# Width of the projection matmuls for the second half of the tokens: 512 columns instead of two groups of 256

## The chip, the cores and the metric

The kernel runs on one core of a Trainium2 chip. The metric is the time of one execution on the device in microseconds (us), given as the median of the runs. The engines are named as in the profile: PE (TensorE, with PEld for its weight loads), DVE (VectorE), ACT (ScalarE), POOL (GpSimd) and SP, whose queue issues nearly all DMAs.

## What is computed

One block of a network on x of 2048 tokens by 1024 features, in float32, cut here to what matters:

```python
h = rms_norm(x, norm_g) * (1.0 + scale) + shift
p = h @ w_in                                  # 2048 x 5960: all projections in one product
(pr, pk, pv, pwd, pad_, z_a, q, ckv, z_b, qi, ki, wi, g_a, g_b) = split(p)   # the first 1664 columns after a token shift
y_a = rwkv7_branch(pr, pk, pv, pwd, pad_, ...)            # a recurrence over the tokens
y_b = dsa_branch(q, ckv, qi, ki, wi, ...)                 # index scores, the best 256 keys, attention over them
br_a = (y_a * silu(z_a)) @ w_pa
br_b = (y_b * silu(z_b)) @ w_pb
merged = sigmoid(g_a) * br_a + sigmoid(g_b) * br_b
out = rms_norm(x + gate * (merged @ w_o), final_g)
```

## The kernel before

The tokens are cut into four blocks of 512 (`TB`), the features of x into eight groups of 128 (`KD`). Operands are split into a high and a low part (`whi`, `wlo` for weights, `hh`, `hl` for the transposed and normed h), and a product is made of three matmuls: high by high, high by low, low by high.

A *unit* of the projection GEMM is one group of 128 output columns for one block of 512 tokens. It fills one PSUM bank `g` (two buffers) with 3 x 8 products. `self.cut` says in how many groups of columns the bank is filled, one group after the other, each with its own accumulation:

```python
        w = TB // self.cut
        for c in range(self.cut):
            s = slice(c * w, c * w + w)
            n = 0
            for k in range(KD):
                for a, b in ((hi, hh), (hi, hl), (lo, hh)):
                    T.matmul(p[:, s], a[:, k], b[:, k, s], start=n == 0, stop=n == 3 * KD - 1)
                    n += 1
```

After a unit, `evacuate` takes the whole bank away: kind "s" (the columns of the recurrence) with ACT L333 and DVE L334, kind "q" with ACT L264 and DVE L265 (`split_out`), the latent columns with `latent` (L356 to L367), and kinds "z" and "g" (gates) with the ACT copy L347 alone. All write to DRAM.

`gemm_half` is called for the first two blocks of tokens with all kinds, and then for the last two with "rkv" (13 groups of columns), "q" (5) and "z", "g" (24). That makes 84 units for the first half, 84 for the second, and 20 more for the index projections (`gemm_index`), which run first.

Around the second half's GEMM stands the recurrence. For each block of tokens, `rwkv_pass` (from L607) prepares factors, `rwkv_inv` inverts triangular blocks on DVE (L733 and the reduction behind it), and `rwkv_chain` (from L742) goes through eight chunks of 64 tokens, each of which needs the state that the one before left: PE L781 and L784, ACT copy L787, PE L790, DVE copy L791, PE L794, DVE L799, PE L801. `heads` (L868, L878) prepares keys and values. After the GEMM, `branch_a` (L1092) makes the first branch's output projection in eight blocks of 256 tokens, and then `attention` and `finish` follow.

The order of instructions on each engine isn't written out by hand. The scheduler of the language sets it when the kernel is built: it goes through the program by an estimated timeline, and of the instructions that are ready on an engine takes that with the lowest number in `self.band(...)`: the passes and inversions of the blocks 0 and 1 and the first chain from 50000, later passes, inversions and chains from 55000, the projections "rkv" 60000, `heads` 65000, the projections "q", "z", "g" 70000, `branch_a` 75000, attention 80000. Weight loads and evacuations go before all else (`urgent`). On the chip each engine then runs its instructions in the order that was set.

Of the kernel before, what the change touches and what calls it, by code (L numbers as in the profile page):

```python
# [25 lines left out]
FR = mybir.dt.float32r  # L26
# [5 lines left out]
PSUM = bass.MemoryType.PSUM  # L32
DRAM = bass.MemoryType.DRAM
# [11 lines left out]
LOWEST = -1.0e38  # L45
# first columns of the projections
C_R, C_K, C_V, C_WA = 0, 512, 1024, 1536
# [4 lines left out]
class Block:  # L52
# [19 lines left out]
    def move(self, dst, src, q=None):  # L72
        """a DMA of float32r words as they are"""
        f = [a.bitcast(FT) if a.dtype == FR else a for a in (dst, src)]
        return (q or self.nc.sync).dma_start(f[0], f[1])
# [3 lines left out]

    # ---------------------------------------------------------------- constants  # L80
    def consts(self):
# [5 lines left out]
        DMA.dma_start(self.ident, x["k_ident"])  # L87
        # scratch in DRAM
        self.QIS = d.tile([8, 128, S], FR, name="qis")
# [21 lines left out]

    # ---------------------------------------------------------------- start: modulation, norm, h^T
    def start(self):
# [32 lines left out]
        for tb in range(NTB):  # L146
# [23 lines left out]
            if tb >= 2:  # L170
                self.move(self.HHS[tb - 2], hh, q=G)
                self.move(self.HLS[tb - 2], hl, q=G)
        # the last third of the modulation is for the end
        acc = self.ada(w, cT, 2, [])
# [7 lines left out]
        DMA.dma_start(self.GT, ab)  # L182
        # bias by distance; beyond the last bucket's start it is constant and drops out of the softmax
        rb, bk, br = (w.tile([32, n], FT, name="b%d" % i, bufs=1) for i, n in enumerate((8, 384, 384)))
# [11 lines left out]
    def ada(self, w, cT, j, ahead):  # L196
        """a third of the modulation, partial sums by partition"""
        nc = self.nc
        acc = w.tile([128, D], FT, name="acc")
        for k in range(KD):  # L200
            aw = w.tile([128, D], FT, name="x", bufs=7)
            m = nc.sync.dma_start(aw, self.x["ada_w"][k * 128:(k + 1) * 128, j * D:(j + 1) * D])
            if j == 0:
                self.shift_in = m.ins
            if k == 0:
                nc.vector.tensor_scalar(acc, aw, cT[:, 0:1], None, op0=OP.mult)
            else:
                nc.vector.scalar_tensor_tensor(acc, aw, cT[:, k:k + 1], acc, op0=OP.mult, op1=OP.add)
            if ahead:
                ahead.pop(0)()  # L210
        return acc

    # ---------------------------------------------------------------- the projection GEMM
    @contextmanager
    def urgent(self):
        """what frees or feeds the tensor engine goes before all else"""
        p = self.tc.cur_priority
# [37 lines left out]
    def split_out(self, p, scale=None, rows=128):  # L255
        """FR hi and lo of a PSUM tile."""
        nc, w = self.nc, self.wp
# [43 lines left out]
    def gemm_half(self, tbs, kinds):  # L301
# [4 lines left out]
        for kind in kinds:  # L306
# [6 lines left out]
            if kind == "g":  # L313
                jobs += [("g", i, C_GA + i * 128) for i in range(16)]
        # at the turn of the halves, a block of tokens serves two columns at a time
        n = len(jobs)
# [53 lines left out]

    # ---------------------------------------------------------------- index scores and the selection
    def select(self):
        """For each query the mask of its TOPK best keys (ties go to the lower index).

        A threshold is sought by the secant method on the count of scores at or above it, until the count is
        at most eight short of TOPK; the missing ones are then the largest below the threshold. Where the
        search has not ended so, a branch finds the TOPK-th largest value bit by bit.
        """
        nc, tc = self.nc, self.tc
        V, A, T, G, DMA = nc.vector, nc.scalar, nc.tensor, nc.gpsimd, nc.sync  # L380
        MID = TOPK - 4.0
        with ExitStack() as ctx:
# [15 lines left out]
            for grp in self.groups:  # L398
# [9 lines left out]
                for g, qb in enumerate(grp):  # L408
# [19 lines left out]
                    V.tensor_tensor(sco[:, n1:n], sco[:, n1:n], tri, op=OP.add)  # L428
                    # a first guess from mean and mean deviation of the keys that all rows see
                    j = w.tile([128, S], BF, name="ja", bufs=1)  # L430
# [9 lines left out]
                for it in range(self.passes):  # L440
                    if it:
                        # next threshold: a step of nothing once the count is near enough
                        d, dd, sl, tn = sm("d"), sm("dd"), sm("sl"), sm("t", bufs=3)
# [14 lines left out]
                    for g, qb in enumerate(grp):  # L458
                        n = 128 * (qb + 1)
                        tg, cg = t[:, g:g + 1], cnt[:, g:g + 1]  # L460
                        if qb in self.on_act and it < self.passes - 1:
                            # with Sign a score equal to the threshold counts half: good enough to go on
                            j = w.tile([128, S], BF, name="ja", bufs=1)
                            A.activation(j[:, :n], sc[g][:, :n], AF.Sign, bias=tg, scale=-1.0, accum_out=cg)
                            V.tensor_scalar(cg, cg, -0.5, n / 2.0, op0=OP.mult, op1=OP.add)
                        else:
                            V.tensor_scalar(hs[g][:, :n], sc[g][:, :n], tg, 0.0, op0=OP.is_ge, op1=OP.add, accum_out=cg)
                # rows that found their threshold
                ok = sm("ok")
# [28 lines left out]
    def select_bits(self, grp, sc, hs, t, cnt, y, eq, w):  # L498
        """The selection for any scores: the TOPK-th largest value bit by bit, ties by prefix sums.

        Leaves 1 for the selected and 0 for the others as scores, and their threshold."""
        V = self.nc.vector
# [22 lines left out]

    # ---------------------------------------------------------------- RWKV-7, chunks of 64
    def rwkv_open(self, ctx):
# [22 lines left out]
        V.tensor_scalar(R["kai"], R["k_a"], -0.5, 1.0, op0=OP.mult, op1=OP.add)  # L550
        # the small second factors: hi twice, and lo
        wa2 = R["ld"].tile([128, 512], FT, name="pk")
# [47 lines left out]
    def parts(self, pool, t):  # L600
        """FR hi and lo of a tile"""
        hi, lo = (pool.tile([128, 512], FR, name=n) for n in ("kk", "ei"))
# [114 lines left out]
    def rwkv_inv(self, tb):  # L717
        """inverses of the unit triangular 32-blocks, one block a partition"""
        nc, R = self.nc, self.R
# [22 lines left out]
    def rwkv_chain(self, tb):  # L742
# [8 lines left out]
        for c in range(8):  # L751
# [14 lines left out]
            DMA.dma_start(t1c[0:32], R["ti"][tb][h8].rearrange("h t s -> t h s"))  # L766
            # off-diagonal block of the inverse
            zp = pc.tile([128, 512], FT, name="zu")
# [50 lines left out]
    def chain_out(self, tb, half, yt, yvar):  # L819
        """group norm and bonus of half a block, with features on partitions"""  # L820
        nc, R = self.nc, self.R
# [19 lines left out]

    # ---------------------------------------------------------------- keys and values of all heads
    def heads(self, ctx):
# [40 lines left out]

    # ---------------------------------------------------------------- attention over the selected keys
    def attention(self):
        nc, tc, x, d = self.nc, self.tc, self.x, self.d
        V, A, T, G, DMA = nc.vector, nc.scalar, nc.tensor, nc.gpsimd, nc.sync
        with ExitStack() as ctx:
# [7 lines left out]
            for h in range(8):  # L897
# [18 lines left out]
                for j in range(NQB // 2):  # L916
                    L = []
                    for qb in (2 * j, 2 * j + 1):
                        if h == 0:
                            # masks  # L920
                            if j:
# [64 lines left out]

    # ---------------------------------------------------------------- gates, output projections, last norm
    def split_weights(self, W, k1, w, names, eng, wide=D, **kw):
        """FR hi and lo of a matrix"""
        nc = self.nc  # L990
# [14 lines left out]
    def gated(self, w, ps, fb, br, li=None, at=None, lb="lb"):  # L1005
        """a branch times silu of its gate, hi and lo"""
        nc = self.nc
# [27 lines left out]
    def zy(self, fb, br, k, z, y):  # L1035
        """a block's gate and the branch itself"""
        tb, qs = fb // 2, slice((fb % 2) * FB, (fb % 2) * FB + FB)
# [11 lines left out]
    def weigh(self, ps, name, tb, li, **kw):  # L1049
        """one over the sums of the softmax, by head, for the queries of a block"""  # L1050
        nc = self.nc
# [8 lines left out]
    def first_loads(self):  # L1060
        """for the second branch's first block, while the last head goes on"""
        h0 = self.hd0
# [17 lines left out]
    def branch(self, w, ps, fb, br, m, wt, u):  # L1080
        """two columns of a branch's projection, gated"""
        nc = self.nc
# [20 lines left out]
    def branch_a(self, fbs):  # L1103
        """the first branch's projection, gated, for blocks that are done early"""
        nc = self.nc
# [82 lines left out]
    def build(self, upto="all"):  # L1188
# [46 lines left out]
        self.band(60000)  # L1235
        self.cut = 2
        self.gemm_half((2, 3), ("rkv",))
# [53 lines left out]
def shape_constants():  # L1291
    """Constants that depend on the shapes alone."""
    import numpy as np
# [13 lines left out]
    import ml_dtypes  # L1307
    # by query: the normal quantile that TOPK of its keys lie above, and the slope there
    quant = np.zeros((128, NQB, 2), f)
# [7 lines left out]
    k["k_causal"] = np.where(t <= s, 0, -BIG).astype(ml_dtypes.bfloat16)  # L1317
    # one-hot of the bucket of distance 255 - column, less that of the last bucket
    dist = 255 - np.arange(384)
# [38 lines left out]
```

## Time and profile before

| | |
|---|---|
| Median of three runs | 2612.31 us (2610.18 to 2612.83) |
| Span of the profiled execution, first to last instruction | 2605.7 us |
| PE busy | 2449.8 us, 94% |
| PEld busy | 2153.8 us, 83% |
| DVE busy | 1750.5 us, 67% |
| ACT busy | 1229.8 us, 47% |
| POOL busy | 868.2 us, 33% |

The busy share of an engine is a mean over stages with different limits, so the table says where to look and not yet what a stage waits for. Of the profiled execution the profile gives the span; the median of the runs lies 6.6 us above it, and that is taken for what lies around the span.

### The profile page before, as it was taken

The numbers are of one execution on the slowest core, as the hardware profiler recorded it, in microseconds if no ns is written. First come the engines' busy times: TensorE is split into PE (matmuls) and PEld (weight loads), VectorE is DVE, ScalarE is ACT, GpSimd is POOL, SyncE is SP. The second block draws the span as 40 slices with busy tenths as digits, with TensorE's granted clock in tenths as the row PEclk, the third lists the DMA queues.
The fourth block names the chain that finished last, engine by engine and source line by source line (L and its number), as shares of the span: only waits on it lengthen the run. The fifth ranks groups of instructions, "written<-read, shape, count | busy, mean of one in ns | idle before, by whom it ended". The sixth has DMA issues, their size and how long they took to land. (4 is left out here: it accounts for less than half of the span.)

```text
span 2605.7 us, 45357 instructions
## 1 busy us (share of the span) xinstructions
PE 2449.8 (94%) x16776; PEld 2153.8 (83%) x16776; DVE 1750.5 (67%) x3509; ACT 1229.8 (47%) x2136; POOL 868.2 (33%) x707
## 2 busy tenths in 40 slices
PE   4899999989899999899999999999989999999998
PEld 3687777868677899689898888988978999988887
DVE  6615888798988355774956947533468888877443
ACT  4315636446344423324334233343367888865332
POOL 2311131241323333223233322131155545645342
PEclk9999999999999999899999999999999999999999
DMA  7754222522233756568677669977763334145442
GB/s 245 271 149 127 77 85 73 131 77 88 84 103 102 243 162 202 147 192 234 179 219 204 187 189 284 293 233 189 239 199 116 91 88 118 45 152 195 147 150 77
DMA packets 423499, 415.69 MB, mean 160 GB/s; under 512 B 80010, under 2 KB 339890, under 8 KB 418404
## 3 DMA queue, kind: packets, MB, share of 16 engines
q1 hardware_dynamic: 422692, 404.33, 51.7%
q0 software_dynamic: 576, 8.39, 0.8%
q8 instruction: 132, 2.16, 0.4%
q14 instruction: 99, 0.81, 0.1%
HBM read 254.04 MB, written 160.15 MB: 159 GB/s over the span
## 5 line engine op out<-in xcount | busy, mean ns | idle before, releaser
L251 PE MATMUL g<-hh,whi 128*128 128x256 f32 (+1 forms) x2176 | 726.9, 334 | 14.8 <-DVE eo L265 4.5
L251 PE MATMUL g<-hl,whi 128*128 128x256 f32 (+1 forms) x2176 | 722.5, 332 | 3.9 <-POOL hl L169 2.4
L251 PE MATMUL g<-hh,wlo 128*128 128x256 f32 (+1 forms) x2176 | 721.0, 331 | 1.2 <-POOL wlo L237 1.2
L251 PEld LDWEIGHTS g<-hh,whi 128*128 128x128 f32 x2176 | 421.4, 194 | 63.8 <-issue 5.7
L251 PEld LDWEIGHTS g<-hl,whi 128*128 128x128 f32 x2176 | 421.0, 193 | 47.6 <-issue 3.9
L251 PEld LDWEIGHTS g<-hh,wlo 128*128 128x128 f32 x2176 | 420.7, 193 | 42.7 <-issue 3.9
L237 POOL TENSOR_TENSOR wlo<-wraw,whi 128x1024 fp32r<-128x1024 f32 (+1 forms) x89 | 216.9, 2437 | 629.4 <-ACT whi L236 583.0
L421 ACT ACTIVATE re<-ixs 128x512 f32<-128x512 f32 (+3 forms) x304 | 158.9, 548 | 176.1 <-DVE sc L427 109.8
L427 DVE SCALAR_TENSOR_TENSOR sc<-re,wi,sc 128x512 f32<-128x512 f32 (+3 forms) x266 | 222.6, 842 | 21.7 <-ACT re L421 6.5
L236 ACT CAST whi<-wraw 128x1024 fp32r<-128x1024 f32 (+1 forms) x89 | 92.8, 1042 | 175.1 <-PE g L251 131.0
L957 PE MATMUL pt<-ident,lt 128*128 128x128 f32 x1088 | 168.2, 276 | 6.4 <-ACT tp L963 3.5
L947 ACT ACTIVATE lt<-lt,nm 128x128 f32<-128x128 f32 (+15 forms) x128 | 154.7, 1211 | 14.2 <-DVE nm L946 14.1
L943 DVE CUSTOM_DVE_ANT_0 lt<-lg,mask 128x512 f32<-128x512 f32 (+3 forms) x256 | 147.4, 590 | 15.9 <-PE lg L941 7.5
L974 PE MATMUL yv<-ph,vp 128*128 128x256 f32 (+1 forms) x576 | 151.5, 285 | 6.7 <-ACT yl L978 4.7
L968 DVE TENSOR_TENSOR pl<-pt,ph 128x512 fp32r<-128x512 f32 (+1 forms) x216 | 139.1, 657 | 25.7 <-ACT ph L967 24.6
L974 PE MATMUL yv<-pl,vp 128*128 128x256 f32 x576 | 152.4, 300 | 2.0 <-POOL pl L965 2.0
L418 PE MATMUL ixs<-kim,st 128*128 128x512 f32 (+3 forms) x304 | 117.3, 387 | 28.7 <-ACT re L421 24.8
L940 PE MATMUL lg<-m,sq 128*128 128x256 f32 (+3 forms) x384 | 137.2, 366 | 5.0 <-DVE cm L943 4.1
L957 PEld LDWEIGHTS pt<-ident,lt 128*128 128x128 f32 x1088 | 125.9, 141 | 15.6 <-ACT tp L963 4.5
L941 PE MATMUL lg<-m,sq 128*128 128x256 f32 (+3 forms) x384 | 127.4, 337 | 0.0
L733 DVE TENSOR_TENSOR prd<-tm,ln 128x1 f32<-128x1 f32 (+30 forms) x124 | 113.3, 914 | 20.5 <-DMA pk<-pj 14.6
L967 ACT CAST ph<-pt 128x512 fp32r<-128x512 f32 (+1 forms) x216 | 115.9, 565 | 19.7 <-PE pt L957 13.7
(347 smaller groups left out, 5391.4 us busy)
## 6 DMA issues: line engine op xcount, KB each, us to landing
wraw<-in_w_in_dram SPq DMA_DIRECT2D x88, 512.0 KB
gg<-eo SPq DMA_DIRECT2D x64, 256.0 KB
gmd<-gt SPq DMA_DIRECT2D x64, 256.0 KB
gmc<-gmd SPq DMA_DIRECT2D x32, 512.0 KB
g<-gg SPq DMA_DIRECT2D x64, 256.0 KB
m<-ks SPq DMA_DIRECT2D x32, 512.0 KB
pj<-eo SPq DMA_DIRECT2D x52, 256.0 KB
x<-in_ada_w_dram SPq DMA_DIRECT2D x24, 512.0 KB
```

Of the source, the lines that this page charges most:

```text
L237: nc.gpsimd.tensor_tensor(lo[:, :, :n], raw[:, :, :n], hi[:, :, :n].bitcast(FT), op=OP.subtract)
L251: T.matmul(p[:, s], a[:, k], b[:, k, s], start=n == 0, stop=n == 3 * KD - 1)
L418: T.matmul(p[:, :kn], st[:, h], M[0][:, k0:k0 + kn], start=True, stop=False)
L421: A.activation(r[:, :kn], p[:, :kn], AF.Relu)
L427: V.scalar_tensor_tensor(o, r[:, :kn], wi, o, op0=OP.mult, op1=OP.add)
L940: T.matmul(p[:, :kn], sq[:, qb * 128:(qb + 1) * 128], m1[:, k0:k1_], start=True, stop=False)
L941: T.matmul(p[:, :kn], sq[:, qb * 128:(qb + 1) * 128], m2[:, k0:k1_], start=False, stop=True)
L943: V.tensor_tensor_reduce(lt[:, k0:k1_], p[:, :kn], mk, 1.0, -3.0e38, OP.add, OP.max, cm[:, i:i + 1])
L947: ex = A.activation(lt[:, :n], lt[:, :n], AF.Exp, bias=nm, accum_out=lsum[:, qb, h:h + 1])
L957: T.transpose(p[:, o:o + 128], L[i][:, kt * 128:(kt + 1) * 128], self.ident)
L968: V.tensor_tensor(pl[:, :n], p[:, :n], ph[:, :n].bitcast(FT), op=OP.subtract)
L974: T.matmul(yv[:, qs], vp[:, kt, :], b[:, o:o + nn], start=kt == 0 and i == 0, stop=kt == last and i == 1, skip_group_check=True)
```

## The change

The line that sets two groups a bank before the second half's GEMM is taken out, so that `self.cut` keeps the value 1 that was set ahead of the first half. The other lines of the diff take comments away and are not shown.

```diff
@@ -1233,7 +1233,6 @@
         self.band(50000)
         self.rwkv_chain(0)
         self.band(60000)
-        self.cut = 2
         self.gemm_half((2, 3), ("rkv",))
         self.band(55000)
         self.rwkv_pass(2)
```

All three later calls of `gemm_half` for the blocks 2 and 3 ("rkv", "q", and "z", "g") run with it.

## Rows read from the trace of the kernel before

**Rows 1.** The page: span, busy time of each engine.

```profile
span 2605.7 us, 45357 instructions
PE 2449.8 (94%) x16776; PEld 2153.8 (83%) x16776; DVE 1750.5 (67%) x3509; ACT 1229.8 (47%) x2136; POOL 868.2 (33%) x707
```

**Rows 2.** Busy time by stretch: engines, granted clock, DMA share, GB/s.

```profile
862.00:1055.00 193.00, 191.08 (x1476) 178.65 (x1475) 93.21 (x140) 69.46 (x104) 71.55 (x50) 1.00 0.65 193
1055.00:1165.00 110.00, 92.71 (x671) 82.72 (x670) 90.73 (x123) 34.11 (x52) 24.79 (x20) 0.91 0.59 163
1165.00:1748.00 583.00, 576.91 (x5512) 526.43 (x5510) 366.11 (x568) 215.71 (x364) 182.57 (x170) 0.99 0.75 224
1832.00:1890.00 58.00, 56.09 (x461) 55.89 (x461) 24.97 (x42) 19.67 (x31) 7.76 (x6) 0.97 0.69 220
1890.00:1965.00 75.00, 60.06 (x408) 54.84 (x407) 51.05 (x171) 49.01 (x97) 37.82 (x46) 0.91 0.67 194
```

**Rows 3.** The same for line L251 alone: PE, PEld, clock, DMA share, GB/s.

```profile
862.00:1055.00 193.00, 161.00 (x1247) 153.41 (x1246) 1.00 0.65 193
1055.00:1165.00 110.00, 69.94 (x493) 64.66 (x491) 0.91 0.59 163
1165.00:1748.00 583.00, 306.46 (x2256) 284.09 (x2256) 0.99 0.75 224
```

**Rows 4.** Groups by shape, L251 at 256 columns: busy us, mean ns | idle before.

```profile
L251 PE MATMUL g<-hh,whi 128*128 128x256 f32 x1344 | 390.9, 291 | 5.8 <-DVE eo L265 4.5 <-DMA hh<-hhs 0.7 <-DVE eo L334 0.5
```

**Rows 5.** Timeline of PE, first half's GEMM: start us, length us.

```profile
499.74 0.39 PE L251 MATMUL g<-hh,wlo 128*128 128x512 f32 x1
...
515.38 0.39 PE L251 MATMUL g<-hh,wlo 128*128 128x512 f32 x1
```

**Rows 6.** Timeline, second half: one chunk's steps with the GEMM between.

```profile
1692.80 1.02 PE L784 MATMUL pp<-uv,gmc 64*64 64x64 f32 x14
1693.86 0.58 ACT L787 COPY xx<-pp 64x512 f32<-64x512 f32 x1 [0.59 <-PE pp L784]
...
1694.09 0.29 PE L251 MATMUL g<-hl,whi 128*128 128x256 f32 x1
...
1696.73 0.28 PE L251 MATMUL g<-hh,wlo 128*128 128x256 f32 x1
1696.94 1.14 PE L790 MATMUL zu<-xx,ttc 64*64 64x64 f32 x16
1698.12 0.68 DVE L791 COPY uv<-zu 64x512 f32<-64x512 f32 x1 [10.05 <-PE zu L790]
...
1701.23 0.94 PE L794 MATMUL hp<-uv,bkc 128*128 128x128 f32 x7
```

**Rows 7.** Waits of PE, 1165 to 1748 us, the longest: total, times, longest.

```profile
PE pg L685 <- ACT kk L603: 1.4, 1, 1.4
PE zu L790 <- ACT xx L787: 1.1, 1, 1.1
```

**Rows 8.** Waits of PE, 1055 to 1165 us, the longest.

```profile
PE pp L784 <- DMA uv<-vtd: 4.8, 1, 4.8
PE g L251 <- DVE eo L265: 4.5, 1, 4.5
PE pg L669 <- DVE nrs L638: 4.5, 1, 4.5
```

**Rows 9.** Busy time at the first and third inversion, columns as in rows 2.

```profile
1055.00:1112.00 57.00, 44.23 (x291) 38.31 (x290) 51.04 (x77) 21.36 (x30) 11.77 (x8) 0.85 0.48 132
1425.00:1480.00 55.00, 54.80 (x524) 50.04 (x525) 54.28 (x68) 16.87 (x30) 17.99 (x16) 0.97 0.58 174
```

**Rows 10.** Lines L781 and L1092: ns min/median/max, first and last start.

```profile
L781 PE MATMUL pp<-H,arc x256: 270/275/377, 1026.7 to 1813.4; 128*128 128x128 f32 x128
L1092 PE MATMUL br<-uh,w_pah x256: 277/281/582, 1752.1 to 1890.2; 128*128 128x256 f32 x128
```

## The prediction

> **What bounds the kernel now.** I read the page first. Over the whole span PE is busy 94% of the time, and the next engine, DVE, 67% [rows 1]. That is a mean, so the second view is the busy time by stretch, cut where the work changes. The second half's GEMM runs from about 855 to 1748 us, in three stretches. From 862 to 1055 us (the projections of the recurrence) PE is busy 191.1 of 193 us. From 1055 to 1165 us (latent columns and queries) it is busy 92.7 of 110, so 17.3 us stand idle. From 1165 to 1748 us (gates) it is busy 576.9 of 583, with 6.1 us idle [rows 2]. The third view is the same cut for L251 alone: the GEMM is 161.0, 69.9 and 306.5 us of these busy times, the rest being the recurrence and the keys and values [rows 3].
>
> A busy PE can still be a PE that follows a slower chain, so the fourth view is the list of PE's waits. In the 583 us of the gates there are six entries, and the longest single wait is 1.4 us [rows 7]. The timeline shows why. In one chunk of the recurrence the ACT copy L787 ends at 1693.86 + 0.58 = 1694.44 us, but L790, which needs it, starts at 1696.94, because GEMM matmuls stand between them in PE's order. The copy L791 ends at 1698.80, and L794 starts at 1701.23 [rows 6]. So each of these two steps has about 2.4 us in hand: it waits for PE's order, not PE for it. In the gates PE sets the pace, and what PE saves there moves everything behind it. From 1055 to 1165 us it is otherwise: PE waits there for DVE evacuations (L265), for factors (L638) and for a DMA, 4.5 to 4.8 us each [rows 8].
>
> Behind the GEMM, from 1832 to 1890 us, PE is busy 56.1 of 58 us with `branch_a`; the last chunk of the recurrence starts at about 1813 us and `branch_a` ends at 1890 [rows 2, 10]. So at the end of the recurrence there is still PE work in hand: an earlier end of the GEMM isn't lost there as long as less than some 50 us are gained.
>
> **The change part by part.** Nothing is added. Every pair of matmuls over 256 columns with the same weights becomes one over 512, with one weight load instead of two.
>
> *How many.* There are three groups of 256-column matmuls, alike in number; one stands, with 1344 [rows 4]. 3 x 1344 = 4032, which is 84 units x 48. They become 2016. By stretch, half of the counts of L251: 623 pairs to 1055 us, 246 to 1165, 1128 to 1748 [rows 3]; the 18 or so left over stand before 862 us.
>
> *What one costs.* The lengths of the instructions overlap and don't add up, so I take the distance from start to start in an unbroken run. In the first half's GEMM, at 512 columns, 69 steps lie between 499.74 and 515.38 us: 15.64 / 69 = 226.7 ns [rows 5]. In the gates, at 256 columns, 22 steps lie between 1694.09 and 1696.73 us: 2.64 / 22 = 120.0 ns [rows 6]. The granted clock is 0.99 to 1.00 in the stretches around, that is the level of 2.4 GHz, where 512 columns alone are 213.3 ns and 256 are 106.7. At both widths some 13.3 ns are left over for each instruction, and the change takes one such remainder out of each pair: 2 x 120.0 - 226.7 = 13.3 ns.
>
> *The sum on PE.* 2016 x 13.3 ns = 26.8 us: 8.3 in the first stretch, 3.3 in the second, 15.0 in the third and 0.2 before.
>
> The Trainium skill, page "TensorE: Matmul & The Clock Gate", section "Back-to-back issue gap", gives for the isolated gap at the full clock the columns over 2.4 GHz plus 2.5 ns, which makes, as an estimate, 109.2 and 215.8 ns, a saving of 2.5 ns a pair and 5.0 us in all. By that rule the change would be at the bound of what can be measured; the rows show 120.0 and 226.7 ns, five times that remainder, and the measurement decides.
>
> *What isn't passed on.* In the second stretch PE waits for others, so I count its 3.3 us as lost; bounds are 0 and 3.3. In the third, PE arrives earlier at each step of the recurrence, and steps that now just come in time become waits. Bounds are 0 and all 15.0. I take half of the idle time that is there now, 6.1 / 2 = 3.1 us, near the low end, since the steps seen have 2.4 us in hand and the GEMM run between two of them shrinks by only 13.3 parts in 240: 5.5% of some 3 us, under 0.2 us.
>
> *What else depends on it.* The evacuation reads the whole bank after its last matmul, as before; a unit takes 24 x 226.7 ns = 5.4 us instead of 5.8, against an ACT copy of about 0.6 us hidden behind the other bank. Weight loads from DRAM and their splits are the same, for two units (10.9 us) each. The DMA share is 0.75 on the mean in the gates [rows 2]; 15 us less makes it 0.77, so the transfers still fit on the mean. From 1890 us on attention starts, with PE busy 60.1 of 75 us; its loads wait for buffers and for `branch_a`, so this start moves with the end of the stage.
>
> *The order.* The scheduler lays out the order anew with another count of instructions, so the interleaving from 855 us on won't be the same one with longer matmuls. The profile can't price that. Bounds: the idle of the second stretch gone (17.3 us better), or the same stall a second and third time (34.6 us worse). I take nothing for the middle.
>
> *The sum.* 2605.7 - 26.8 + 3.3 + 3.1 = 2585.3 us for the span. The median of the runs lies 6.6 us above the span shown, so 2591.9, or **2592 us**.
>
> **The rivals.** A difference of 0.2%, 5.2 us, is about what a measurement of this kernel can tell from none: 2607.1 and 2617.5 us are the borders.
>
> *A, slower: the evacuations fall behind the inversions.* Each of four inversions fills DVE for about 55 us (51.0 of 57 and 54.3 of 55 in the two that stand; the other two are like the later one). During the first, PE is busy only 44.2 of 57 us; during the third, 54.8 of 55 [rows 9]. The difference is what PE has in hand: gate units are evacuated by ACT alone, while the query units need L265 on DVE, which is queued behind the inversion [rows 8]. If the new order sets units or factors that need DVE beside a later inversion, the second stretch's idle comes again there. One more time costs 17.3 us and leaves a gain of 3; from the second more on it decides: 34.6 - 26.8 + 6.4 = 14.2 us worse, 2626 us. Such a stall can be shorter than the first, or come a third time, so I take 2612 to 2632 us, with 2620 as its value. For it: it happened once, and the order is new. Against it: three inversions of four passed without it.
>
> *B, the gain is absorbed.* The recurrence is serial, and if its steps bind, PE's 15.0 us in the gates turn to idle time, as may the 8.3 ahead of the stall. Then between 4 and 12 us are left: 2600 to 2608, in the worst case nothing, with 2606 us as its value. For it: the idle in the second stretch. Against it: the 2.4 us in hand at two steps, and waits of 6.1 us in 583.
>
> *C, the remainder isn't saved.* The 226.7 ns are from a run that had PE to itself; among the small matmuls of the recurrence and heavier DMA traffic a 512-column matmul could cost as much as two of 256, 240.0 ns. Then the time is 2612 us. Against it: the 120.0 ns stand in just such a stretch and show the same remainder of 13.3 ns as the quiet one, so it looks like a part of the instruction and not of the surroundings. The skill's rule above, with 5.0 us, would end in the same place.
>
> **How the numbers follow.** Forecast (2578 to 2600 us): 0.50. A: 0.29, of which 0.03 stays within 0.2%. B: 0.18, of which 0.05 is still faster by over 0.2% and 0.13 within. C: 0.03, within. Faster 0.50 + 0.05 = 0.55; same 0.13 + 0.03 + 0.03 = 0.19; slower 0.26. The likeliest time is 2592 us. Its own range is 2578 (the whole 26.8 us and half of the idle of the second stretch) to 2600. The range for 8 in 10 takes in B, C and most of A: 2578 to 2628 us.
>
> **What the profile after would show.** L251 with 2016 matmuls of 512 columns more and none of 256, at 226.7 ns from start to start in the second half too: if it is 240, C is right. PE's busy time 27 us less, and the end of L251 near 1728 instead of 1748 us. PE's waits between 1055 us and the end of the gates: 20 to 27 us for the forecast, 35 or more for B, 55 or more with DVE lines as releasers for A. The end of `branch_a` near 1870 us, and from there to the end of the span the same 715 us; if that last part differs by more than 5 us, something that I don't name here decides. The prediction is wrong if PE's idle time takes the place of its busy time, or if the new order is worse by more than the 26.8 us.

## The result and the profile after

The kernel became slower: 2702.11 us, median of four runs (2701.86 to 2711.22), against 2611.24 us before on the same chip. The ratio is 1.036, with a 95% interval of 1.0336 to 1.0384. The forecast was 2592 us, the range ended at 2628. A profile shows one execution, and single executions lie up to some 15 us off their median: the one shown of the kernel after is the slowest of its four, the one of the kernel with 512 columns in the order of before (further down) the fastest of twelve.

The page of the kernel after, span, engines and granted clock in 40 slices, to be held against [rows 1]:

```profile
span 2709.5 us, 41352 instructions
...
PE 2503.7 (92%) x14760; PEld 2094.4 (77%) x14760; DVE 1750.3 (65%) x3509; ACT 1234.0 (46%) x2138; POOL 870.3 (32%) x707
...
PEclk9999999999999999989989986678989999999999
```

PE has 2016 matmuls fewer, as it should, and yet 53.9 us more busy time (2503.7 against 2449.8). Its idle time grew too, from 155.9 to 205.8 us. Both together are the 103.8 us by which the span grew. Busy time that grows while work shrinks points at the clock: it dips to 6 to 8 tenths in the slices 24 to 28 (about 1560 to 1900 us).

Lines L251, L781 (the first step of each of the 32 chunks of the recurrence) and L1092 (`branch_a`) of the kernel after, with the first and last start; the two latter answer to [rows 10]:

```profile
L251 PE MATMUL g<-hh,wlo x1504: 387/389/795, 46.5 to 1594.6; 128*128 128x512 f32 x188
...
L781 PE MATMUL pp<-H,arc x256: 270/275/582, 1072.4 to 1938.2; 128*128 128x128 f32 x128
...
L1092 PE MATMUL br<-uh,w_pal x256: 276/281/420, 1839.3 to 1992.6; 128*128 128x256 f32 x128
```

The GEMM ends at 1594.6 us, 153 us earlier than before (1747.8), where some 20 us were forecast. The recurrence, though, starts 46 us later and its last chunk begins 125 us later. What follows `branch_a` takes 716.9 us, as before (715.5). So the loss lies between 862 us and the end of the recurrence, and these numbers point at a GEMM that was done too early at the recurrence's cost; the experiments test that.

How this came about shows in the number of GEMM matmuls that stand between two chunks. L251 alone in three neighbouring chunk steps (chunks 9 to 11, from L781 to the next L781) and, in the last row of each, from the start of chunk 17 to the end of the recurrence, first before, then after; columns are the length, PE and PEld busy with counts, clock, DMA share, GB/s:

```profile
1324.90:1342.10 17.20, 8.21 (x62) 7.59 (x62) 1.00 0.84 255
1342.10:1357.40 15.30, 5.02 (x37) 4.62 (x38) 1.00 0.70 211
1357.40:1374.10 16.70, 7.51 (x59) 6.93 (x57) 1.00 0.72 206
1504.60:1831.70 327.10, 130.94 (x968) 121.95 (x968) 0.97 0.80 240
```

```profile
1414.10:1436.10 22.00, 12.66 (x53) 9.72 (x53) 1.00 0.64 191
1436.10:1456.50 20.40, 10.61 (x44) 7.84 (x43) 1.00 0.52 149
1456.50:1478.90 22.40, 12.83 (x53) 9.27 (x51) 1.00 0.69 213
1643.50:1956.60 313.10, 0.00 (x0) 0.00 (x0) 0.78 0.82 246
```

The scheduler laid nearly as many matmuls between two chunks as before, 53, 44 and 53 against 62, 37 and 59, but each is now twice as wide. (Over the chunks 2 to 15 it is 901 against 1078.) These three steps take 21.6 us on the mean instead of 16.4, and the GEMM is used up before the last 17 of 32 chunks. Beside the last 16 there is none, where 968 matmuls of 256 columns stood before.

What it looks like there: PE's longest waits from 1602 to 1957 us, total, times and longest, and a step of the chain on the timeline:

```profile
PE pg L685 <- ACT kk L603: 9.4, 1, 9.4
PE hp L794 <- DVE uv L791: 7.1, 7, 2.1
PE p L878 <- DVE v L882: 4.2, 3, 2.4
```

```profile
1610.28 1.96 PE L790 MATMUL zu<-xx,ttc 64*64 64x64 f32 x16
```

PE now waits for the copy L791, which had time in hand before [rows 6]. And the 16 matmuls of L790 take 1.96 us where they took 1.14 [rows 6]: that is nearly the factor of two between the clock levels of 2.4 and 1.2 GHz, so they ran for the most part at the lower one.

### The profile page after: what moved, and what is told of

Read it like the earlier page. It is cut to its first block, busy times and chain, and to the rows that moved or that the text cites. A ratio compares the mean times of both kernels' runs of the same rounds, so it can differ in the third digit from the quotient of the medians.

```text
span 2709.5 us, 41352 instructions
## 1 busy us (share of the span) xinstructions
PE 2503.7 (92%) x14760; PEld 2094.4 (77%) x14760; DVE 1750.3 (65%) x3509; ACT 1234.0 (46%) x2138; POOL 870.3 (32%) x707
## 5 line engine op out<-in xcount | busy, mean ns | idle before, releaser
L251 PE MATMUL g<-hh,whi 128*128 128x512 f32 x1504 | 611.5, 407 | 26.5 <-DVE eo L334 5.7
L251 PE MATMUL g<-hl,whi 128*128 128x512 f32 x1504 | 606.1, 403 | 3.2 <-POOL hl L169 2.3
L251 PE MATMUL g<-hh,wlo 128*128 128x512 f32 x1504 | 604.9, 402 | 0.0
L251 PEld LDWEIGHTS g<-hh,whi 128*128 128x128 f32 x1504 | 291.2, 194 | 102.0 <-ACT eo L347 6.8
L251 PEld LDWEIGHTS g<-hl,whi 128*128 128x128 f32 x1504 | 290.8, 193 | 68.9 <-POOL hl L169 3.1
L251 PEld LDWEIGHTS g<-hh,wlo 128*128 128x128 f32 x1504 | 290.5, 193 | 64.5 <-issue 3.3
```

## The experiments

Theory 1: the order makes the loss, since GEMM work stands ahead of chunks that it needn't delay. Rival, theory 2: the width itself does, by a longer matmul in front of each small step or by the lower clock that goes with it. A later question was how much of the loss the half clock accounts for.

### GEMM units tied to the chunks, and one part wide

The first two kernels hold each gate unit, at 512 columns, behind the chunk in which it began before (`GATES` lists that chunk for each unit; the first line stands in `paced`); the second also holds the 36 units ahead of the gates behind steps of the passes.

```diff
+        return self.tc.issue_after(self.chunks[GATES[n - 36]])
...
-                    p = self.unit(wt, tb)
+                    with self.paced(tbs):
+                        p = self.unit(wt, tb)
```

> All of the second half at 512 columns. Each of the 48 gate units is queued on PE behind the chunk of the recurrence in which it began in the kernel before, so the GEMM can't run ahead of the recurrence; the units of the recurrence's and the queries' columns stay as the scheduler puts them. Theory 1 (order: between two chunks the scheduler lays as many matmuls of 512 columns as it laid of 256, so the GEMM is used up early and the recurrence is left alone on a PE at half clock): the time comes back to 2595 us, 2580 to 2620. Theory 2 (a 512-column matmul costs more than it saves among the recurrence's small matmuls, by clock or contention): it stays near 2700 us.

> As e1, and the 36 units ahead of the gates are held behind the steps of the first two passes in the same way, so that the order is that of the kernel before throughout, with 512-column matmuls. Theory 1: PE's saving of 26.8 us comes through, 2592 us, 2580 to 2605, under e1 by 0 to 20 us. Theory 2: near 2700 us.

Measured: 2673.44 us (ratio 1.024, 1.0223 to 1.0257) and 2657.33 us (1.0189, 1.0164 to 1.0214). Both lie far above theory 1's ranges. Spreading the units took back 29 and 45 of the 91 us. That speaks for the order, but half of the loss stayed, although the GEMM now lasts into chunk 27 of 32; so that it runs out early isn't the whole loss. A unit tied as a whole still lies in one clump, and between the clumps the granted clock falls. The second kernel, in two neighbouring stretches of 20 us with 47 and 4 GEMM matmuls:

```profile
1400.00:1420.00 20.00, 19.56 (x111) 14.97 (x109) 4.46 (x8) 5.53 (x9) 4.48 (x6) 0.94 0.47 136
1420.00:1440.00 20.00, 14.06 (x79) 10.72 (x80) 11.09 (x20) 9.45 (x16) 3.54 (x3) 0.57 0.59 179
```

The next two have only one part wide, the units "rkv" and "q" (the diff shown) or the gates:

```diff
         self.band(70000)
+        self.cut = 2
         self.gemm_half((2, 3), ("z", "g"))
```

> Only the projections of the recurrence and of the queries at 512 columns; the gates in two groups of 256 as before. Theory 1: the front runs ahead of the first passes, the gates are used up some 6 chunks before the recurrence ends instead of 17; 2640 us, 2615 to 2670, with the half clock only in those last chunks. Theory 2, by share (864 of 2016 pairs): 2650 us, with no stretch at half clock that the order explains. This run tells how the loss is divided, not which theory holds.

> The reverse of e3: only the gates at 512 columns. Theory 1: the first chunks start as in the kernel before (second one near 1171 us), the gates are used up some 10 chunks before the recurrence ends; 2650 us, 2625 to 2680. Theory 2, by share (1152 of 2016 pairs): 2663 us. With e3 this divides the loss.

Measured, one run each: 2636.75 us with the gates at 256 columns and 2648.33 us with only the gates at 512, against 2609.87 before. Each part loses, 27 and 38 us; together they lose more (91) than the sum. So no single kind of unit is the cause. Both times lie in theory 1's ranges, but theory 2's 2650 and 2663 us are only 13 and 15 us above them, which single runs hardly tell apart.

### The same order on PE, by one tie for each matmul

Each wide matmul is held behind the instruction that stood in front of the second half of its pair (the first line stands in `behind`).

```diff
+        return self.tc.issue_after(self.laid[self.row[n]])
...
+                    with self.behind(n, tb):
+                        m = T.matmul(p[:, s], a[:, k], b[:, k, s], start=n == 0, stop=n == 3 * KD - 1)
```

> All of the second half at 512 columns, and each of its 2016 matmuls queued on PE behind the instruction that stood in front of the second matmul of its pair in the kernel before. e1 and e2 paced the GEMM by whole units and still left PE stretches without GEMM, at half clock; this keeps the fine interleaving. Theory 1 (only the order makes the loss): 26.8 us less than the kernel before on PE, less some new waits: 2590 us, 2580 to 2606, granted clock as before (0.97 or more on the mean). Theory 2 (the wide matmul itself costs among the small ones): above 2640 us with the mixture the same, and the loss shows as longer steps between chunks at full clock.

Measured: 2634.25 us (ratio 1.0083, 1.0055 to 1.0111), which misses the expectation, though it is 68 us below the kernel after. The tie is a lower bound only: by the trace, at least a sixth of PE's 7650 other instructions in this part of the program stand elsewhere than before. So it was no clean test of the width; the next pair is.

### Width and order apart

All five queues (PE, DVE, ACT, POOL, SP) are pinned to a list by edges from each instruction to the next. The first kernel has 512 columns in the order of before, where a wide matmul stands in the place of the second of its pair. The second has 256 columns in the order of after, both halves of a pair where the wide one stood.

```diff
+        for e in PINNED:
+            row = [by[e][k] if k >= 0 else self.mine[-k - 1] for k in ORDER[e]]
+            for a, b in zip(row, row[1:]):
+                self.tc.add_manual_dep(b, a.name, info, reason="pin")
```

> All of the second half at 512 columns, with the instruction order of every engine pinned to that of the kernel before: each 512-column matmul stands where the second matmul of its pair stood, and all other instructions of PE, DVE, ACT, POOL and SP follow one another as there. In e5 only the GEMM was held back and the rest was laid anew; about a quarter of PE's other instructions stood elsewhere. If the order makes the whole loss (theory 1), PE's saving comes through here: 2588 us, 2575 to 2602. If the width itself costs, by clock or by waits (theory 2), the time is at or above the kernel before, 2608 to 2640 us.

> The reverse: two groups of 256 columns as in the kernel before, with the order of every engine pinned to that of the kernel after (two 256-column matmuls in the place of each of 512). Theory 1: the loss of the kernel after and the 26.8 us that its wide matmuls saved: 2729 us, 2715 to 2745, with the stretch from about 1620 us on at a granted clock of 0.6 to 0.7 as there. Theory 2: most of the loss is gone, 2610 to 2660 us.

| us | order of before | order of after | order costs |
|---|---|---|---|
| 256 columns | 2611.8 | 2720.7 | +108.9 |
| 512 columns | 2603.5 | 2702.1 | +98.6 |
| width gives | -8.3 | -18.6 | |

The ratios to before are 0.9974 (0.996 to 0.9989) for wide in the old order and 1.0438 (1.0407 to 1.0469) for narrow in the new one. The edits did what they say: in the trace of the first, all but 2 of PE's 7650 other instructions stand in their old place, and the second has twice the GEMM matmuls of the kernel after beside each chunk. 2720.7 us is in theory 1's range; 2603.5 lies 1.5 us above it and 4.5 below theory 2's, so the width gave less than forecast, but it did give. Theory 2 falls: the width saves time in either order. The order alone costs about 100 us, at either width. Wide matmuls in the old order are faster than both kernels. That pinning by itself costs nothing is not shown: neither kernel was run pinned to its own order with nothing else changed. The pin takes in all five queues, so the pair shows that the order makes the loss; which part of the order is read from the profiles below and from the ties above.

With the same instructions in both orders, the loss can be laid out. Busy time of all engines in the kernel with 512 columns in the old order, cut at the first chunk, at chunk 17 of 32 and at the end of the recurrence:

```profile
0.00:1017.40 1017.40, 931.67 (x4035) 737.89 (x4036) 722.43 (x1333) 451.52 (x766) 274.91 (x142) 0.97 0.45 138
1017.40:1492.00 474.60, 447.00 (x3121) 352.78 (x3119) 336.54 (x501) 169.70 (x274) 159.70 (x138) 0.97 0.69 199
1492.00:1815.40 323.40, 313.35 (x2568) 263.68 (x2566) 160.57 (x264) 117.43 (x203) 77.59 (x76) 0.98 0.82 243
1815.40:2594.60 779.20, 738.18 (x5043) 674.81 (x5042) 525.48 (x1411) 489.50 (x894) 355.22 (x352) 0.98 0.43 131
```

The same four stretches of the kernel after:

```profile
0.00:1072.40 1072.40, 973.51 (x4218) 773.03 (x4219) 744.45 (x1355) 470.93 (x790) 286.59 (x148) 0.97 0.45 136
1072.40:1643.60 571.20, 540.47 (x3422) 431.86 (x3420) 324.87 (x479) 176.06 (x281) 172.34 (x142) 0.92 0.61 173
1643.60:1956.60 313.00, 276.97 (x2311) 240.65 (x2310) 168.91 (x286) 111.06 (x196) 61.23 (x71) 0.78 0.82 246
1956.60:2709.50 752.90, 712.75 (x4816) 648.83 (x4814) 512.07 (x1390) 475.97 (x871) 350.12 (x348) 0.97 0.41 125
```

Up to chunk 17 the kernel after runs 7640 PE instructions, the other 7156: 484 more. The old order has just 484 GEMM matmuls beside the last 16 chunks, about 110 us at 228 ns. Chunk 17 starts 151.6 us later (1643.6 against 1492.0): those 110 us, some 25 us by which PE's busy time grew beyond them, and 16.3 us more idle time. Behind that point the 110 us are gone from PE's work, but only 36.7 us come back (10.4 in the chunks, 26.3 behind them). The difference, 114.9 us, is the loss between these two executions (98.6 us by the medians, so the parts are rather too large): 73.5 us of PE busy time, at a clock of 0.92 and 0.78 in the two middle stretches instead of 0.97 and 0.98, and 41.4 us of idle time.

### Useless matmuls beside the last chunks

Is it the half clock that keeps the 110 us from coming back? Matmuls of 512 columns whose results are overwritten were added to the chunks without GEMM. At first by the scheduler's own order, eight in each of the last 16 chunks, four of them by these lines (`FILL` is 4) and four by two like them ahead of L794:

```diff
+            for h in range(FILL if tb >= 2 else 0):
+                T.matmul(up, R["w2"][:, 0:128], R["w2"], start=True, stop=True)
```

> The kernel after, with eight more 512-column matmuls in each of the last 16 chunks of the recurrence, which then has no GEMM beside it; their results are overwritten, so they are work without use, 16 x 8 x 0.227 = 29 us of PE at full clock. If the half clock makes those chunks slow (theory 1a): the granted clock from 1600 to 1850 us rises from about 0.65 to 0.9 or more, and although work is added the time falls, 2660 us, 2640 to 2690. If the waits of the recurrence for the other engines and DMAs set its pace (theory 1b): the clock may rise, but the time stays or rises, 2700 to 2731 us.

Measured: 2719.68 us (ratio 1.0426, 1.0392 to 1.0461). The last chunk started at 1907.6 us, 29 us earlier, although 29 us of work were added. But the scheduler moved `branch_a` too, and the stretch behind the recurrence grew from 773 to 807 us from the last chunk's start on. The whole time therefore tells nothing; the test was made again with the order of after pinned, and 8 or 28 such matmuls in each of the chunks 17 to 27 (88 and 308, that is 20 and 70 us; the old order has 484 GEMM matmuls beside the last 16 chunks).

> The kernel after with the order of every engine pinned to its own, and eight added 512-column matmuls in each of the chunks 17 to 27 of the recurrence, four ahead of L790 and four ahead of L794; their results are overwritten. 88 x 0.227 = 20 us of work at full clock. In e6 the scheduler also moved the output projection to a later place, so its time told nothing; here nothing is moved. Theory 1a (half clock makes these chunks slow): granted clock from 1600 to 1850 us at 0.85 or more, the last chunk starts 25 to 45 us earlier than in the kernel after, time 2665 us, 2650 to 2690. Theory 1b (waits on other engines and DMAs make them slow): the last chunk at the same place or up to 20 us later, 2700 to 2722 us.

> The same with 28 added matmuls in each of these chunks, about as much as the GEMM had there in the kernel before: 308 x 0.227 = 70 us of work at full clock. Theory 1a: it rides along, since each step has time in hand and the clock stays up: 2705 us, 2685 to 2725. Theory 1b: it adds its work, 2760 us, 2745 to 2775.

Three windows beside these chunks, in the kernel after, in the one with 8 a chunk, and in that with 28:

```profile
1602.00:1700.00 98.00, 85.35 (x617) 71.72 (x617) 58.51 (x87) 27.04 (x47) 30.47 (x33) 0.62 0.60 175
1700.00:1800.00 100.00, 83.57 (x561) 65.47 (x560) 77.19 (x135) 30.27 (x56) 11.07 (x15) 0.72 0.85 257
1800.00:1850.00 50.00, 39.27 (x338) 33.94 (x338) 14.79 (x23) 20.63 (x34) 12.26 (x13) 0.62 0.98 295
```

```profile
1602.00:1700.00 98.00, 85.15 (x654) 69.19 (x653) 60.83 (x92) 28.57 (x50) 32.41 (x33) 0.76 0.63 183
1700.00:1800.00 100.00, 82.33 (x597) 63.91 (x595) 74.72 (x131) 29.52 (x56) 11.10 (x14) 0.81 0.85 260
1800.00:1850.00 50.00, 40.67 (x376) 34.20 (x377) 16.15 (x24) 21.52 (x37) 12.82 (x14) 0.80 0.93 287
```

```profile
1602.00:1700.00 98.00, 87.64 (x593) 72.09 (x593) 48.35 (x73) 22.83 (x39) 23.57 (x26) 0.73 0.53 152
1700.00:1800.00 100.00, 95.56 (x729) 77.48 (x727) 62.16 (x116) 25.89 (x48) 16.39 (x21) 0.91 0.67 197
1800.00:1850.00 50.00, 37.54 (x213) 27.43 (x213) 29.37 (x42) 13.31 (x25) 1.53 (x3) 0.80 0.90 269
```

Measured: 2707.58 us (ratio 1.0372, 1.0347 to 1.0397) and 2744.04 us (1.0506, 1.0477 to 1.0535), 5.5 and 42 us above the kernel after. The clock rose, from 0.62, 0.72 and 0.62 in these windows of the kernel after to 0.76, 0.81 and 0.80 with 8, less than the 0.85 that was expected. Of 20 us of added work about 15 cost nothing, of 70 us about 28. PE's busy time over the whole span tells how: with 20 us added it is 2501.6 us and with 70 us 2551.3, against 2503.7 in the kernel after, so about 22 us of busy time were given back in either; idle time is 207.2 and 196.2 us against 205.8, so only with 28 a chunk some 10 us of the added work ran in idle time. So the half clock has a part in the loss, of some 22 of the 98.6 us as far as this could raise it. As far as the clock was raised, the theory that it is the whole isn't borne out; a full clock in all of these chunks wasn't reached.

### The same work left out at two places

If the chain of the last 16 chunks has a pace of its own, GEMM beside it must be nearly free. In the old order at 512 columns, 22 of 24 matmuls were left out of each of 11 units (242 matmuls, 55 us), once among the projections ahead of the recurrence, once beside the last 16 chunks. Loads from DRAM, evacuations and the rest of the order stay.

```diff
+                    if self.second and len(self.mine) // 24 in OUT and 0 < n < 23:
+                        self.mine.append(None)
+                        n += 1
+                        continue
                     m = T.matmul(p[:, s], a[:, k], b[:, k, s], start=n == 0, stop=n == 3 * KD - 1)
```

> 512 columns in the order of before, with 22 of the 24 matmuls of 11 units left out (242 matmuls of 512 columns, 55 us of PE at 227 ns), in the projections of the recurrence, ahead of the second chunk; weight loads, evacuations and transfers stay. The same order with all matmuls took 2603.5 us. Theory 1 (GEMM ahead of the recurrence's chunks delays them one for one, GEMM beside the last chunks rides along): 40 to 55 us less, 2548 to 2564 us. Rival (PE is the bound in both places, and the loss of the new order comes from its lower clock and its waits): the same 40 to 55 us less. Under 30 us less, the stage ahead of the chunks has another bound than PE, its transfers (DMA share 0.66) before all, and theory 1 falls too.

> The same with 11 of the last 20 units: again 242 matmuls, 55 us of PE, but these stand beside the last 16 chunks of the recurrence. Theory 1: the chunks take nearly as long without them, 5 to 20 us less, 2583 to 2598 us. Rival: the same saving as with the early units left out, 40 to 55 us less, 2548 to 2564 us. In the profile theory 1 has PE's idle time in the last 16 chunks up by 35 us or more, or a lower granted clock there; the rival has neither.

Measured: 2592.58 us early (ratio 0.9942, 0.9907 to 0.9978) and 2590.66 us late (0.9927, 0.9903 to 0.995), 10.9 and 12.8 us less than the 2603.5 of the kernel with all matmuls.

Late: a hit for theory 1. The last 16 chunks of that kernel:

```profile
1496.60:1814.80 318.20, 285.14 (x2344) 239.76 (x2341) 162.32 (x266) 116.94 (x204) 80.72 (x76) 0.88 0.83 248
```

318.2 us instead of 323.4: of 55 us left out, 5.2 came back there in the executions shown (2600.2 us against 2596.4); the median of the whole gives 12.8 us. PE's idle time rose from 10.1 to 33.1 us, and the clock fell from 0.98 to 0.88, though order, loads and evacuations stayed. So of the 55 us at most some 13 are paid for beside these chunks, and taking GEMM away is also what lowers the clock.

Early: a miss, and by the words of that expectation (under 30 us less) theory 1 falls in its sharp form, that GEMM ahead of the chunks costs one for one. The stage from 862 us, first with all matmuls, then with those left out, and what PE waits for in the latter (L258 is the GEMM's line there, L344 an evacuation's, L695 and L613 belong to the pass):

```profile
862.00:1017.00 155.00, 154.22 (x700) 118.54 (x698) 79.87 (x120) 58.46 (x88) 56.03 (x40) 0.99 0.61 185
862.00:1017.00 155.00, 125.55 (x509) 90.04 (x508) 85.71 (x129) 60.95 (x92) 58.50 (x42) 0.87 0.67 201
```

```profile
PE g L258 <- DVE eo L344: 8.8, 3, 3.9
PE pg L695 <- ACT kk L613: 8.3, 3, 4.4
```

PE is idle for 29.5 of 155 us, where all matmuls leave 0.8; it waits for the evacuations on DVE and for the factors on ACT. In the old order this stage stands where PE and the other engines bind at once: work taken away from PE gives little. That work which is added there, as by the new order, costs one for one is read from the 151.6 us by which chunk 17 starts later, and no run tested it by itself. The two savings, 10.9 and 12.8 us, lie within each other's intervals, so the whole time doesn't tell the two places apart. Nor do the profiles by much: with the early units left out chunk 17 starts 9.0 us earlier (1483.0 against 1492.0), with the late ones the last 16 chunks are 5.2 us shorter.

## Why the prediction was wrong

**The step that failed is the one headed "The order."** The sum put it at nothing. It said that the order would be laid out anew and that the profile couldn't price that, set bounds of 17.3 us better and 34.6 us worse from the idle time of one stretch, and took nothing. The order cost 98.6 us at this width, nearly three times the bad bound. That the new order is worse by more than the 26.8 us is the last of the signs of being wrong that the prediction named. The bounds were drawn from the wrong place. Something to go by stood in the rows: between two chunks the scheduler lays runs of GEMM matmuls, 22 steps in the run of [rows 6], and the time in hand of about 2.4 us was read there as a margin. Had the run kept its count and each matmul its new length, chunk steps would have grown and the GEMM would have ended far ahead of the recurrence. That the scheduler treats a 512-column matmul about as a 256-column one is read from the counts (53, 44, 53 against 62, 37, 59); its estimate of either wasn't changed in a run, so this link is argued, not shown.

**The saving of PE, 26.8 us, was too large.** With the order held, PE's busy time fell by 19.6 us (2449.8 to 2430.2), of which idle time took back 8.5; by the medians 8.3 us were passed on, by the ratio 6.8 (2.9 to 10.4). The GEMM's line in that kernel (L253 there), in the three stages of [rows 3]:

```profile
862.00:1049.00 187.00, 152.57 (x611) 112.52 (x609) 0.99 0.66 196
1049.00:1152.00 103.00, 67.55 (x244) 47.65 (x244) 0.89 0.58 163
1152.00:1731.00 579.00, 296.57 (x1128) 206.64 (x1128) 0.99 0.77 225
```

In the gates, the last stage, both kernels have 1128 pairs: 296.6 us against 306.5, 8.8 ns a pair and not 13.3, 9.9 us instead of 15.0. In the two stages ahead it is 220.1 us against 230.9, but over 855 pairs against 870, since 15 more stand before 862 us there; they make some 3.4 us of the difference. Together the GEMM saved about 17 us, 8.7 ns a pair. The reason shows where a run of GEMM begins behind another instruction, on the timeline of that kernel and then of the kernel before:

```profile
1677.70 0.50 PE L253 MATMUL g<-hh,wlo 128*128 128x512 f32 x1
1678.04 0.39 PE L253 MATMUL g<-hh,whi 128*128 128x512 f32 x1
...
1680.55 0.39 PE L253 MATMUL g<-hh,wlo 128*128 128x512 f32 x1
```

```profile
1693.75 0.39 PE L251 MATMUL g<-hh,wlo 128*128 128x256 f32 x1
1693.97 0.28 PE L251 MATMUL g<-hh,whi 128*128 128x256 f32 x1
1694.09 0.29 PE L251 MATMUL g<-hl,whi 128*128 128x256 f32 x1
```

The first wide matmul holds the place for 0.34 us. Before, the two narrow ones of such a first pair took 0.22 and 0.12 us: the same. Over all runs of GEMM in the gates the median from the first pair's start to the next is 340 ns before and 335 ns with 512 columns, so the first pair saves next to nothing; the others do, at (1680.55 - 1678.04) / 11 = 228 ns against 240. And of what PE saved, the waits of the chain took more than the 3.1 us set down for the gates: the idle time there rose from 6.1 to 11.6 us.

The 6.6 us between span and median were not what lies around the span: in every run on record the time is 1.7 to 1.9 us above its own span, and the rest is that the execution shown was shorter than the median. The forecast isn't touched by it, since the sum only carries the difference along.

By the Trainium skill, page "TensorE: Matmul & The Clock Gate", section "Back-to-back issue gap", the estimate in the prediction was a saving of 5.0 us. The 8.3 us of the medians, what is left after waits, are nearer to it than to 26.8, but not for its reason: the GEMM alone saved about 17 us, and the remainder is 228 - 213.3 = 15 ns here, not 2.5.

**Rival A** has the right sign and the wrong mechanism: PE's longest wait for L265 from 1055 to 1602 us is 2.6 us. **Rival B** names the right actor, the serial recurrence, but as something that can only absorb a gain; with GEMM beside it gone it absorbed most of the 110 us that were freed, after they had been paid for ahead of it. **Rival C** is out: 228 to 229 ns in the gates of the kernel after, too.

**The signposts.** No 256-column matmul of the GEMM is left, the pace is as said, and behind `branch_a` the time is the same. PE's idle time from 1072 to 1602 us is 21.2 us (125.07 us busy of 141 and 383.72 of 389), inside the 20 to 27 of the forecast; that it held says nothing for the forecast, since the stage is laid out otherwise. PE's busy time should have been 27 us less and was 53.9 us more. The end of L251 near 1728 us and of `branch_a` near 1870 were missed, by 133 us early and 123 us late. The kernel pinned to the old order met both: 1730.4 and 1872.9 us. From there to its end it took 721.7 us, 6 us more than before, and no run tells why.

**What stays open.** Of the 73.5 us of longer PE busy time the added matmuls won back some 22; how much more a full clock throughout would give wasn't tried, since what was added to raise it also lies in the chain's way. That the last 16 chunks hardly get shorter with less GEMM on PE is shown by the work left out late, at a clock that fell with it; which step of the chain binds isn't shown. That the order makes the loss is shown; that the GEMM's place in it does, and not the other engines' order, rests on the tied kernels, which took back 29, 45 and 68 of the 91 us, and on the account by stretch.

## What to carry to other kernels

Where a scheduler lays out the order when the kernel is built, changing the size of an instruction also changes the order, and that can outweigh what the instruction saves: here 8 to 19 us against 99 to 109. Count how many filler instructions stand between the steps of a serial chain, before and after, and see that the filler lasts to the chain's end; a GEMM that finishes early beside a chain is a warning. To last is not enough: tied by whole units it lasted into chunk 27 and still lost 47 to 64 us. Judge a width with the order pinned; here that gave the fastest version.

## What the hardware showed beside this

Without GEMM beside it, the recurrence ran on a PE that the profile shows busy most of the time and that was yet granted little more than half of its clock. In the kernel after:

```profile
1602.00:1750.00 148.00, 130.34 (x901) 109.21 (x902) 90.67 (x160) 40.28 (x71) 37.65 (x41) 0.60 0.65 189
1750.00:1850.00 100.00, 77.85 (x614) 61.92 (x612) 59.82 (x86) 37.66 (x66) 16.16 (x19) 0.74 0.97 296
```

From 1602 to 1750 us PE is busy 88% of the time by the profile and is granted 0.60 of the clock. (The busy share is taken with the matmuls as long as they are at that clock.) In the old order, with GEMM beside the chain, the last 16 chunks had 0.98 at 512 columns and 0.97 at 256. Leaving out half of that GEMM brought 0.88. So the GEMM beside the chain also keeps up the clock of its small matmuls, which a sum of durations at the full clock doesn't show.
